# Combining attention heads in parts, and retention outputs one slot later, in a hybrid transformer block

## The chip, the cores and the metric

One core of one Trainium2 chip. The metric is the device time in microseconds of the program, lower is better. An execution's time has a span, from the first to the last instruction that the profiler shows, and a little around it.

## What is computed

One block of a decoder on x of 1 x 1024 x 1024, in fp32. Cut to what matters here:

```python
xn = rmsnorm(x, norm1_g)
qa, ka, va, qr, kr, vr, gr, gate_a, gate_b = split(xn @ w_in)
# mixer A: 12 heads of 128 = 3 groups (dilation 1, 4, 16) x 4 head slots
for gi, (window, dilation) in enumerate(ATT_GROUPS):
    o, lse = dilated_group(qa[gi], ka[gi], va[gi], slopes[gi], window, dilation)
alpha = softmax(stack(lses), axis=0)                 # over the three groups
o_a = sum(alpha[..., None] * stack(outs), axis=0)    # 1024 x 512: one head per slot
# mixer B: 4 heads, q and k of 256, v of 512, in 8 chunks of 128 rows
s = einsum('bnqhd,bnkhd->bnhqk', qc, kc) * decay     # within the chunk
inner = einsum('bnhqk,bnkhv->bnqhv', s, vc)
cross = q_i @ state                                  # from the chunks before
state = state * g_chunk + kz_i.T @ v_i
o_r = head_groupnorm(inner + cross, ret_gn_g, ret_gn_b) * silu(gr)
y = sigmoid(gate_a) * (o_a @ w_proj_a) + sigmoid(gate_b) * (o_r @ w_proj_b)
x = x + y @ w_out
x = x + square(relu(rmsnorm(x, norm2_g) @ w_up)) @ w_down
```

## The kernel before

**Products.** Each fp32 operand is split into a high part, rounded to TensorE's fp32r format by ScalarE (L287), and the rest, computed by VectorE (L288). A product is three matmuls a term: high by high, low by high, high by low; all stand in one helper and show as L193. Nearly all of TensorE's time goes there.

**Slots.** `Pipe.step` emits one such group of matmuls, a slot. Other functions are due at a slot (`pipe.at(lag, fn)`); `step` spreads those due over its terms, so the small matmuls and transposes of earlier rows stand between the large ones, and the engines beside TensorE have time for what lies between. TensorE executes in the order in which the program is traced. On VectorE (DVE), ScalarE (ACT) and SyncE (SP, whose queue issues the DMAs) a list scheduler sets the order from dependencies, buffers and modelled times; `tc.keep_in_program_order(ins)` ties an instruction to the one traced before it on its engine.

**Attention.** 12 heads, one group of one slot each, in the order of the list `heads`: groups 0, 1, 2 for the first three slots and 1, 2, 0 for the last. A head is 8 slots of TensorE, one for a block of 128 rows (8 terms, 24 matmuls of 128x384 for q, k and v). Behind a block: ScalarE sums the squares, VectorE and GpSimd make 1/rms (ssa, L296 and L297), VectorE scales q and k (qk, L601), TensorE turns them a slot later (tr, L607), and ScalarE and VectorE copy them to qT and kT (L611). `attend` adds scores (L532), Exp on ScalarE (pr, L539), the turn of it (L545), pT (L547) and the values (L552, L554). It runs 2 slots behind the block for group 0, which needs only near rows, and 9 slots behind for the groups 1 and 2, whose rows are regrouped by dilation: these end in the next head. The result `acc` of a head, with its maximum and sum, is stored to acc_d in DRAM (L560 to L566) when its last block is done.

**Combination.** When all three groups of a slot are in DRAM, `load_heads` loads half of the rows as four DMAs into `at` (L400), which has one buffer; `combine` makes the weights w (L408 to L419, with an Exp on ScalarE at L412) and mixes the groups into oa (L422, L424, three instructions for each of four blocks of 128 rows); `turn` transposes it, and it is stored to oa_d. For the slots 0 to 2 this happens in the heads 5, 8 and 11: the halves are traced at the blocks 0 and 3, each with all its instructions at once, the first load at block 6 of the head before and the second right behind the first half. Slot 3 is combined in the first head of retention, at the chunks 1 and 4.

**Retention.** 4 heads of 8 chunks. A slot computes v of a chunk (8 terms of three 128x512 matmuls), split into vh and vl. Due in the next slot: `output` (the scores s by v, then q by the state; L193 on ms), its group norm (L799 to L804) and `update` (two matmul groups into ms, then the state St at L816 and its split Sh, Sl); `decay` of the slot's own chunk is due there too (scores, times the mask at L771, split into smh and sml; q into qh, ql; k turned and scaled into kzh, kzl). `turn_o` is due one slot later: it turns the output, gates it by sr (L831) and stores it to on_d. The mask, the scales rc and the norm's gain gng are loaded at the start of this phase (L724 to L729).

**pa.** Behind retention, the combined attention output is multiplied by w_proj_a: 16 slots of 4 terms, each result gated by s, loaded from sg_d (L870) into a ring of four buffers, multiplied (L888) and stored to pa_d (L889). Here `load_o` loads the rows of on_d (oraw, two buffers) and splits them: four rows at the start, four at once as soon as nothing is due any more.

Of the kernel before, what the change touches and what calls it, by code (L numbers as in the profile page):

```python
# [237 lines left out]
def hybrid_block(ctx: ExitStack, tc: tile.TileContext, a: dict, out: bass.AP):  # L238
# [53 lines left out]
    ident = const.tile([P, P], F, name="ident")  # L292

# [10 lines left out]
    heads = [(slot, g) for slot in range(SLOTS) for g in ((0, 1, 2) if slot < SLOTS - 1 else (1, 2, 0))]  # L304
# [91 lines left out]
    def load_heads(s, i, p2b):  # L396
        at = p2b.tile([P, 4, 3, DH + 2], F, name="at", bufs=1)
        rows = acc_d[512 * i:512 * i + 512].rearrange("(t p) (g s) e -> s p t g e", p=P, s=SLOTS)
        for t in range(4):
            nc.sync.dma_start(at[:, t], rows[s, :, t])  # L400
        return at

    def combine(s, i, p2b, at):

        w = p2b.tile([P, 6, 4], F, name="w")
        nm = [at[:, :, g, DH] for g in range(3)]
        dn = [at[:, :, g, DH + 1] for g in range(3)]
        nc.vector.tensor_tensor(w[:, 5], nm[0], nm[1], op=OP.min)  # L408
        nc.vector.tensor_tensor(w[:, 5], w[:, 5], nm[2], op=OP.min)
        for g in range(3):  # L410
            nc.vector.tensor_tensor(w[:, g], w[:, 5], nm[g], op=OP.subtract)
        nc.scalar.activation(w[:, 0:3], w[:, 0:3], AF.Exp)  # L412
# [7 lines left out]
        oa = p2b.tile([P, 4, DH], F, name="oa")  # L420
        for t in range(4):
            nc.vector.tensor_scalar(oa[:, t], at[:, t, 0, :DH], w[:, 0, t:t + 1], None, op0=OP.mult)  # L422
            for g in (1, 2):
                nc.vector.scalar_tensor_tensor(oa[:, t], at[:, t, g, :DH], w[:, g, t:t + 1], oa[:, t],  # L424
                                               op0=OP.mult, op1=OP.add)

        def turn():
            pt = tr.tile([P, 4, P], F, name="tr")
            for t in range(4):
                nc.tensor.transpose(pt[:, t, :], oa[:, t, :], ident)  # L430
            ot = p2b.tile([P, 512], F, name="oaT")
            nc.scalar.activation(ot, pt.rearrange("p t q -> p (t q)"), AF.Copy)
            nc.sync.dma_start(oa_d[s, :, 512 * i:512 * i + 512], ot)

        return turn
# [6 lines left out]
    with ExitStack() as ph:  # L442
# [69 lines left out]
        for head, (slot, g) in enumerate(heads):  # L512
# [57 lines left out]
            for b in range(NT):  # L570
# [8 lines left out]
                if head in (4, 7, 10) and b == 6:  # L579
                    at = load_heads(head // 3 - 1, 0, cmb)  # L580
                if head in (5, 8, 11) and b in (0, 3):
                    pipe.at(3, combine(head // 3 - 1, b // 3, cmb, at))
                    if b == 0:
                        at = load_heads(head // 3 - 1, 1, cmb)
# [133 lines left out]
    with ExitStack() as ph:  # L718
# [4 lines left out]
        maskT = cp.tile([P, RH, P], F, name="maskT")  # L723
        nc.sync.dma_start(maskT, a["c_mask"])  # L724
        rc = const.tile([P, 3, RH], F, name="rc")
        nc.sync.dma_start(rc, a["c_ret"])

        gng = cp.tile([P, 2, NF], F, name="gng")
        nc.sync.dma_start(gng, a["ret_gn"])  # L729
        ready = {}  # L730

        def load_chunk(n):
# [8 lines left out]
            sr = p2.tile([P, 4, P], F, name="sr", bufs=3)  # L741
# [13 lines left out]
        for h in range(RH):  # L755
# [4 lines left out]
            for c in range(NT):  # L760
# [5 lines left out]
                def decay(c=c, h=h, it=it, qT=qT, kT=kT):  # L766
# [5 lines left out]
                    it["s"] = p2.tile([P, P], R, name="smh"), p2.tile([P, P], R, name="sml")  # L772
                    split(*it["s"], sm)
                    if c > 0:
                        it["q"] = p2.tile([P, 2, P], R, name="qh"), p2.tile([P, 2, P], R, name="ql")
                        split(*it["q"], qT)
                    if c < NT - 1:
# [3 lines left out]
                        kzh = p2b.tile([P, 2, P], R, name="kzh")  # L781
                        kzl = p2b.tile([P, 2, P], R, name="kzl")
# [57 lines left out]
                it["v"] = p2.tile([P, DV], R, name="vh"), p2.tile([P, DV], R, name="vl")  # L840
# [13 lines left out]
    with ExitStack() as ph:  # L854
# [21 lines left out]
        load_o(oS, 0)  # L876
        for d in range(KT):
            ua, = W.take(1)
            uh, ul = W[ua]
            for cs in halves():  # L880
# [9 lines left out]
                if ES is None and not pipe.due:  # L890
# [3 lines left out]
                    load_o(as_rows(ES[0]) + as_rows(ES[1]), 4)  # L894
# [313 lines left out]
```

## Time and profile before

| | us |
|---|---|
| median of three runs | 2324.09 (2323.64 to 2328.1) |
| the profiled execution | 2327.33 |
| its span | 2325.6 |
| TensorE (PE) busy | 2281.0 |
| VectorE (DVE) busy | 1165.8 |
| ScalarE (ACT) busy | 926.2 |
| mean granted TensorE clock | 0.995 |

How to read what follows: a row of the timeline gives start, duration, engine, line, operation, out<-in, shape, and in brackets the time that the engine was idle before it and what released it. A row of a group gives, behind the first bar, total busy time and the mean of one in ns, and behind the second the idle time before the group and its releasers. A row of windows gives a stretch from:to and its length, then busy time (and instructions) of PE, PEld, DVE, ACT and POOL, the granted TensorE clock, the DMA engines' share and GB/s. SPq is SyncE's queue issuing a DMA.

### The profile page before, as it was taken

Reading aid. Unit: us, or ns where it says so; the run is one execution under the profiler, and the core shown is the slowest. Engines: PE = TensorE matmul, PEld = TensorE weight load, DVE = VectorE, ACT = ScalarE, POOL = GpSimd, SP = SyncE. Lnnn points to the kernel's source line nnn. Section 1 sums busy time; section 2 is a strip of 40 time slices with the busy share of each in tenths; the row PEclk is TensorE's granted clock in tenths of the full one; section 3 lists DMA queues with packets and bytes.
Section 4 is the critical chain, followed back from the end, with each engine's and each line's share of the span. In section 5 each row is a group of like instructions: output and inputs, shape, how many; then the busy total and the mean of one; then the engine's idle time right before and its main releaser. Section 6 shows DMA issues by size and latency. Waiting matters only on the chain. (4 is left out here: it accounts for less than half of the span.)

```text
span 2325.6 us, 29822 instructions
## 1 busy us (share of the span) xinstructions
PE 2281.0 (98%) x11060; PEld 1952.9 (84%) x11060; DVE 1165.8 (50%) x2356; ACT 926.2 (40%) x2078; POOL 104.0 (4%) x148
## 2 busy tenths in 40 slices
PE   8999999999999999989999999999999999999999
PEld 7999998998888888868888878888788888888887
DVE  6344445454644445557676752363855555233532
ACT  6444444445343333335455533122566666211010
POOL 1111111110000000000000000000000000000000
PEclk9999999999999999999999999999999999999999
DMA  4212322332233333363433385554254457733601
GB/s 140 82 55 74 105 63 78 96 105 91 68 112 112 117 113 109 100 187 104 123 113 100 104 273 180 164 171 163 83 173 166 167 169 271 288 127 133 234 28 73
DMA packets 186275, 303.19 MB, mean 130 GB/s; under 512 B 13457, under 2 KB 99601, under 8 KB 182034
## 3 DMA queue, kind: packets, MB, share of 16 engines
q1 hardware_dynamic: 186130, 301.29, 39.9%
q8 instruction: 87, 1.43, 0.3%
q14 instruction: 58, 0.48, 0.1%
HBM read 204.68 MB, written 96.57 MB: 130 GB/s over the span
## 5 line engine op out<-in xcount | busy, mean ns | idle before, releaser
L193 PE MATMUL mm<-wh,xh 128*128 128x384 f32 (+1 forms) x1536 | 605.1, 394 | 5.1 <-ACT wh L287 5.1
L193 PE MATMUL mm<-wh,xl 128*128 128x384 f32 (+1 forms) x1536 | 561.7, 366 | 2.4 <-DVE xl L288 2.1
L288 DVE TENSOR_TENSOR wl<-raw,wh 128x1024 fp32r<-128x1024 f32 (+2 forms) x282 | 306.6, 1092 | 423.1 <-ACT wh L287 420.1
L193 PE MATMUL mm<-wl,xh 128*128 128x384 f32 (+1 forms) x1344 | 486.6, 362 | 2.6 <-DVE wl L288 2.6
L287 ACT ACTIVATE wh<-raw 128x1024 fp32r<-128x1024 f32 (+2 forms) x282 | 267.2, 953 | 535.7 <-PE mm L193 272.1
L193 PEld LDWEIGHTS mm<-wh,xh 128*128 128x128 f32 x1536 | 291.5, 190 | 36.6 <-ACT wh L287 5.7
L193 PEld LDWEIGHTS mm<-wh,xl 128*128 128x128 f32 x1536 | 290.4, 189 | 35.5 <-DVE xl L288 3.4
L193 PE MATMUL mm<-xl,wh 128*128 128x512 f32 x848 | 309.7, 390 | 1.7 <-DVE xl L288 1.7
L193 PE MATMUL mm<-xh,wh 128*128 128x512 f32 x848 | 310.1, 390 | 0.0
L193 PE MATMUL mm<-xh,wl 128*128 128x512 f32 x720 | 280.7, 390 | 0.0
L193 PEld LDWEIGHTS mm<-wl,xh 128*128 128x128 f32 x1344 | 256.3, 191 | 24.8 <-DVE wl L288 3.1
L193 PE MATMUL ms<-xh,wh 128*128 128x512 f32 x604 | 238.6, 395 | 3.9 <-DVE s L888 3.8
L193 PE MATMUL ms<-xh,wl 128*128 128x512 f32 x604 | 235.4, 390 | 0.0
L193 PE MATMUL ms<-xl,wh 128*128 128x512 f32 x604 | 235.3, 390 | 0.0
L193 PEld LDWEIGHTS mm<-xl,wh 128*128 128x128 f32 x848 | 159.5, 188 | 35.2 <-DVE xl L288 2.1
L193 PEld LDWEIGHTS mm<-xh,wh 128*128 128x128 f32 x848 | 159.6, 188 | 33.0
L1109 DVE TENSOR_TENSOR Yd<-Yd,mm 128x512 f32<-128x512 f32 x112 | 76.9, 686 | 172.3 <-PE mm L193 172.0
L193 PEld LDWEIGHTS mm<-xh,wl 128*128 128x128 f32 x720 | 135.4, 188 | 28.1
L193 PEld LDWEIGHTS ms<-xh,wh 128*128 128x128 f32 x604 | 113.5, 188 | 30.1 <-DVE s L888 4.2
L193 PEld LDWEIGHTS ms<-xh,wl 128*128 128x128 f32 x604 | 113.4, 188 | 23.8
L193 PEld LDWEIGHTS ms<-xl,wh 128*128 128x128 f32 x604 | 113.5, 188 | 22.4
L539 ACT ACTIVATE pr<-s,acc 128x128 f32<-128x128 f32 (+1 forms) x96 | 43.1, 449 | 149.2 <-DVE acc L537 136.9
(187 smaller groups left out, 2756.4 us busy)
## 6 DMA issues: line engine op xcount, KB each, us to landing
h_d<-hs SPq DMA_DIRECT2D x64, 512.0 KB, 3.9
raw<-in_w_att SPq DMA_DIRECT2D x48, 384.0 KB, 3.9
raw<-in_w_up SPq DMA_DIRECT2D x32, 512.0 KB, 3.9
raw<-in_w_down SPq DMA_DIRECT2D x32, 512.0 KB, 4.4
xh<-h_d SPq DMA_DIRECT2D x12, 1024.0 KB, 7.1
xl<-h_d SPq DMA_DIRECT2D x12, 1024.0 KB, 8.7
sg_d<-sg SPq DMA_DIRECT2D x32, 256.0 KB, 2.0
raw<-in_w_rqk_q SPq DMA_DIRECT2D x16, 512.0 KB, 3.6
```

Of the source, the lines that this page charges most:

```text
L193: self.nc.tensor.matmul(ps, x, y, start=start, stop=stop, skip_group_check=not first)
L287: nc.scalar.activation(dst_h, src, AF.Copy)
L288: nc.vector.tensor_tensor(dst_l, src, dst_h.bitcast(F), op=OP.subtract)
L539: nc.scalar.activation(st["p"][:, :n], s[:, :n], AF.Exp, bias=acc[:, b, DH:DH + 1], accum_out=acc[:, b, DH + 1:DH + 2])
L1109: nc.vector.tensor_tensor(Y[:, t, ns], Y[:, t, ns], pm, op=OP.add)
```

## The change

Three things.

**Attention.** The groups run in the order 1, 2, 0 in every slot, so group 0, with its short lag, is last. The combination becomes a list of parts: `weigh` (all of w), four `mix` (one block of 128 rows each), and `turn_mixed`. For a finished slot the first half is loaded at block 6 of the first head of the next slot and the second at block 6 of the second head; `weigh` of the halves is traced at block 1 of the second and of the third head, and one part follows in each block (`mix_next`). The four loads, the first instruction of `weigh` and the first of each `mix` are kept in program order. For slot 3 the same happens in the retention heads 0 and 1 (load at chunk 1, parts from chunk 3).

**Retention.** `output` and `update` are due a slot later, and so is `turn_o` (two for the last two chunks). sr gets four buffers instead of three, and smh, sml, qh, ql, kzh, kzl, vh, vl three instead of two. The mask, rc and gng move to the pool that is kept throughout, with their loads traced right behind attention; a tile `rest` is reserved and not used.

**pa.** `load_o` loads one row in each slot from a list `waiting`, which the second four rows join when nothing is due any more.

```diff
-    heads = [(slot, g) for slot in range(SLOTS) for g in ((0, 1, 2) if slot < SLOTS - 1 else (1, 2, 0))]
+    heads = [(slot, g) for slot in range(SLOTS) for g in (1, 2, 0)]
...
-            nc.sync.dma_start(at[:, t], rows[s, :, t])
+            tc.keep_in_program_order(nc.sync.dma_start(at[:, t], rows[s, :, t]))
...
+        st = {}
+        return [lambda: weigh(p2b, at, st), *(lambda t=t: mix(t, at, st) for t in range(4)),
+                lambda: turn_mixed(s, i, p2b, st)]
+
+    def weigh(p2b, at, st):
+        w = st["w"] = p2b.tile([P, 6, 4], F, name="w")
+        st["o"] = p2b.tile([P, 4, DH], F, name="oa")
...
-        nc.vector.tensor_tensor(w[:, 5], nm[0], nm[1], op=OP.min)
+        tc.keep_in_program_order(nc.vector.tensor_tensor(w[:, 5], nm[0], nm[1], op=OP.min))
...
+    def mix(t, at, st):
+        w, oa = st["w"], st["o"]
+        tc.keep_in_program_order(
+            nc.vector.tensor_scalar(oa[:, t], at[:, t, 0, :DH], w[:, 0, t:t + 1], None, op0=OP.mult))
+        for g in (1, 2):
+            nc.vector.scalar_tensor_tensor(oa[:, t], at[:, t, g, :DH], w[:, g, t:t + 1], oa[:, t],
+                                           op0=OP.mult, op1=OP.add)
...
+    mixing = []
+
+    def mix_next():
+
+        if mixing:
+            mixing.pop(0)()
+            if len(mixing) == 1:
+                pipe.at(1, mixing.pop())
...
-                if head in (4, 7, 10) and b == 6:
-                    at = load_heads(head // 3 - 1, 0, cmb)
-                if head in (5, 8, 11) and b in (0, 3):
-                    pipe.at(3, combine(head // 3 - 1, b // 3, cmb, at))
-                    if b == 0:
-                        at = load_heads(head // 3 - 1, 1, cmb)
+                if head >= 3:
+                    i = head % 3
+                    if i < 2 and b == 6:
+                        at = load_heads(head // 3 - 1, i, cmb)
+                    if i > 0 and b == 1:
+                        mixing = combine(head // 3 - 1, i - 1, cmb, at)
+                    mix_next()
...
+    nc.sync.dma_start(maskT, a["c_mask"])
+    nc.sync.dma_start(rc, a["c_ret"])
+    nc.sync.dma_start(gng, a["ret_gn"])
...
-                pipe.at(0, output, update)
-                pipe.at(1, turn_o)
-                if h == 0 and c in (0, 2):
-                    at = load_heads(SLOTS - 1, c // 2, p2b)
-                if h == 0 and c in (1, 4):
-                    pipe.at(3, combine(SLOTS - 1, c // 4, p2b, at))
+                pipe.at(1, output, update)
+                pipe.at(2 if h < RH - 1 or c < NT - 2 else 3, turn_o)
+                if h < 2:
+                    if c == 1:
+                        at = load_heads(SLOTS - 1, h, p2b)
+                    if c == 3:
+                        mixing = combine(SLOTS - 1, h, p2b, at)
+                    mix_next()
...
-        load_o(oS, 0)
+        waiting = [(place, n) for n, place in enumerate(oS)]
...
-                    load_o(as_rows(ES[0]) + as_rows(ES[1]), 4)
+                    waiting += [(place, 4 + n) for n, place in enumerate(as_rows(ES[0]) + as_rows(ES[1]))]
+                if waiting:
+                    place, n = waiting.pop(0)
+                    load_o([place], n)
```

Where this moves instructions, at three places. VectorE in the head after a finished slot, around the first instruction of w (L408 before, L419 after; ssa and qk belong to a block of that head, kT to the block before it). Before:

```order
L611 TENSOR_SCALAR kT<-tr,gk 128x4x32
L296 TENSOR_SCALAR ssa<-ssa 128x2
L601 TENSOR_TENSOR qk<-mm,ssa 128x256
L408 TENSOR_TENSOR w<-at 128x4
L409 TENSOR_TENSOR w<-w,at 128x4
L411 TENSOR_TENSOR w<-w,at 128x4 x2
```

VectorE at the same place, after:

```order
L622 TENSOR_TENSOR qk<-mm,ssa 128x256
L632 TENSOR_SCALAR kT<-tr,gk 128x4x32
L419 TENSOR_TENSOR w<-at 128x4
L420 TENSOR_TENSOR w<-w,at 128x4
L300 TENSOR_SCALAR ssa<-ssa 128x2
L422 TENSOR_TENSOR w<-w,at 128x4 x3
L622 TENSOR_TENSOR qk<-mm,ssa 128x256
L424 TENSOR_TENSOR w<-w,at 128x4
```

The first instruction of w stood behind a block's qk, and now stands ahead of a block's ssa and qk.

SyncE's queue, around the load of the mask; at the start of retention before (sr_d, rqT, rkT: stores and loads of retention's operands; raw: weights; oar, at: attention's outputs):

```order
L693 DMA sr_d<-sg 128x512
L740 DMA rqT<-rqk_d 128x2x128
L146 DMA raw_9497<-in_w_rv 128x1024
L693 DMA sr_d<-sg 128x512
L740 DMA rkT<-rqk_d 128x2x128
L752 DMA oar<-oa_d 128x1024
L724 DMA maskT<-in_c_mask 128x512
L729 DMA gng<-in_ret_gn 128x32
L400 DMA at<-acc_d 128x3x130 x4
```

SyncE's queue around the same load after, which is at the kernel's start (xt: rows of x):

```order
L146 DMA raw_263<-in_w_att 128x768
L146 DMA raw_269<-in_w_att 128x768
L478 DMA xt<-in_x 128x1024 x3
L650 DMA maskT<-in_c_mask 128x512
L651 DMA rc<-in_c_ret 128x12
L652 DMA gng<-in_ret_gn 128x32
L146 DMA raw_647<-in_w_att 128x768
```

The constants have left the start of retention and stand behind the first rows of x.

VectorE at the end of retention (xh, xl from oraw: the split of rows of on_d; on, st: the norm of an output; onT: its gating). Before:

```order
L288 TENSOR_TENSOR vl<-mm,vh 128x512
L288 TENSOR_TENSOR xh<-oraw,xh 128x1024
L288 TENSOR_TENSOR xl<-oraw,xl 128x1024
L831 TENSOR_TENSOR onT<-onT,sr 128x512
L799 BN_STATS st<-on 128x6
L800 BN_AGGR st<-st 128x2
L801 TENSOR_SCALAR st<-st,rc 128x1
L803 TENSOR_SCALAR st<-st,rc 128x1
L804 TENSOR_SCALAR on<-on,st 128x512
```

VectorE at the end of retention, after (L835 is St, L850 onT, L818 to L822 the norm):

```order
L288 TENSOR_TENSOR vl<-mm,vh 128x512
L288 TENSOR_TENSOR xh<-oraw,xh 128x1024
L850 TENSOR_TENSOR onT<-onT,sr 128x512
L818 BN_STATS st<-on 128x6
L288 TENSOR_TENSOR xl<-oraw,xl 128x1024
L819 BN_AGGR st<-st 128x2
L835 SCALAR_TENSOR_TENSOR St<-St,ms 128x512
L820 TENSOR_SCALAR st<-st,rc 128x1
L835 SCALAR_TENSOR_TENSOR St<-St,ms 128x512
L822 TENSOR_SCALAR st<-st,rc 128x1
L288 TENSOR_TENSOR Sl<-St,Sh 128x512
```

The last update of the state (L835 and Sl) now stands behind the last vl, among the splits of the rows of on_d.

More of the change, by code (lines that the diff above doesn't have):

```diff
@@ L292, in hybrid_block @@
     ident = const.tile([P, P], F, name="ident")
+    maskT = const.tile([P, RH, P], F, name="maskT")
+    rc = const.tile([P, 3, RH], F, name="rc")
+    gng = const.tile([P, 2, NF], F, name="gng")
+    const.tile([P, 224], F, name="rest")
     def rsqrt(dst, src, scale):
@@ L419, in combine, with turn_mixed @@
             nc.vector.tensor_tensor(w[:, g], w[:, g], w[:, 4], op=OP.mult)
-        oa = p2b.tile([P, 4, DH], F, name="oa")
-        for t in range(4):
[L422 to L435, printed above, removed]
+    def mix(t, at, st):
[5 more added lines that the diff above has]
+                                           op0=OP.mult, op1=OP.add)
+    def turn_mixed(s, i, p2b, st):
+        pt = tr.tile([P, 4, P], F, name="tr")
+        for t in range(4):
+            nc.tensor.transpose(pt[:, t, :], st["o"][:, t, :], ident)
+        ot = p2b.tile([P, 512], F, name="oaT")
+        nc.scalar.activation(ot, pt.rearrange("p t q -> p (t q)"), AF.Copy)
+        nc.sync.dma_start(oa_d[s, :, 512 * i:512 * i + 512], ot)
+    mixing = []
[4 more added lines that the diff above has]
+                pipe.at(1, mixing.pop())
     attn = ExitStack()
@@ L721, in hybrid_block @@
         p2b = pool(ph, "p22b", 2, "right")
[L723 to L729, printed above, removed]
         ready = {}
@@ L740, in load_chunk @@
                 nc.sync.dma_start(qk[i], rqk_d[h, i, :, :, ts].rearrange("f p t -> p f t"))
-            sr = p2.tile([P, 4, P], F, name="sr", bufs=3)
+            sr = p2.tile([P, 4, P], F, name="sr", bufs=4)
             nc.sync.dma_start(sr, sr_d[4 * h:4 * h + 4, :, ts].rearrange("f p t -> p f t"))
@@ L771, in decay @@
                     nc.vector.tensor_tensor(sm, sp[:, :P], maskT[:, h, :], op=OP.mult)
-                    it["s"] = p2.tile([P, P], R, name="smh"), p2.tile([P, P], R, name="sml")
+                    it["s"] = p2.tile([P, P], R, name="smh", bufs=3), p2.tile([P, P], R, name="sml", bufs=3)
                     split(*it["s"], sm)
                     if c > 0:
-                        it["q"] = p2.tile([P, 2, P], R, name="qh"), p2.tile([P, 2, P], R, name="ql")
+                        it["q"] = p2.tile([P, 2, P], R, name="qh", bufs=3), p2.tile([P, 2, P], R, name="ql", bufs=3)
                         split(*it["q"], qT)
@@ L780, in decay @@
                             nc.tensor.transpose(pt[:, f, :], kT[:, f], ident)
-                        kzh = p2b.tile([P, 2, P], R, name="kzh")
-                        kzl = p2b.tile([P, 2, P], R, name="kzl")
+                        kzh = p2b.tile([P, 2, P], R, name="kzh", bufs=3)
+                        kzl = p2b.tile([P, 2, P], R, name="kzl", bufs=3)
                         nc.scalar.activation(kzh, pt[:, :2], AF.Copy, scale=rc[:, 2, h:h + 1])
@@ L839, in hybrid_block @@
                     pm = values(us, ts, c == NT - 1)
-                it["v"] = p2.tile([P, DV], R, name="vh"), p2.tile([P, DV], R, name="vl")
+                it["v"] = p2.tile([P, DV], R, name="vh", bufs=3), p2.tile([P, DV], R, name="vl", bufs=3)
                 split(*it["v"], pm)
-                pipe.at(0, output, update)
-                pipe.at(1, turn_o)
-                if h == 0 and c in (0, 2):
-                    at = load_heads(SLOTS - 1, c // 2, p2b)
-                if h == 0 and c in (1, 4):
-                    pipe.at(3, combine(SLOTS - 1, c // 4, p2b, at))
+                pipe.at(1, output, update)
[6 more added lines that the diff above has]
+                    mix_next()
                 if h == RH - 1 and c >= 4:
@@ L893, in hybrid_block @@
                     ES = [slot_of(ext) for _ in range(3)] + [slot_of(pool(e1, "ext1", 1, "right"))]
-                    load_o(as_rows(ES[0]) + as_rows(ES[1]), 4)
+                    waiting += [(place, 4 + n) for n, place in enumerate(as_rows(ES[0]) + as_rows(ES[1]))]
+                if waiting:
+                    place, n = waiting.pop(0)
+                    load_o([place], n)
+        assert not waiting
         other = places + as_rows(ES[2]) + as_rows(ES[3])
@@ L1196 @@
     from concourse.bass_utils import run_bass_kernel_spmd as _run
-    nc = _bacc.Bacc("TRN2", target_bir_lowering=False, num_devices=1)
+    nc = _bacc.Bacc("TRN2", target_bir_lowering=False, num_devices=1, dynamic_dma_scratch_size=1024)
     arrays, aps = {}, {}
```

1 line of the change is left out of this document (removed).

## The prediction

> **What bounds the kernel now.** I read the page first, then the busy time by stretches of 100 us, then TensorE's own timeline at the places where it falls short, and last the clock in narrow stretches there. Of the page, the span and the engines:
>
> ```profile
> span 2325.6 us, 29822 instructions
> PE 2281.0 (98%) x11060; PEld 1952.9 (84%) x11060; DVE 1165.8 (50%) x2356; ACT 926.2 (40%) x2078; POOL 104.0 (4%) x148
> ```
>
> TensorE (PE) is busy 2281.0 of 2325.6 us: 44.6 us of idle time, and what half clock costs, are all that an edit of order can win. Busy time by stretch (columns: sum, PE, PEld, DVE, ACT, POOL, granted clock, DMA share, GB/s) shows where that lies:
>
> ```profile
> 200.00:300.00 100.00, 96.92 (x583) 94.48 (x582) 44.10 (x174) 40.25 (x165) 12.46 (x18) 0.98 0.32 91
> 300.00:400.00 100.00, 95.22 (x580) 92.41 (x579) 44.74 (x180) 39.74 (x167) 12.45 (x18) 0.98 0.26 72
> 400.00:500.00 100.00, 96.86 (x584) 93.79 (x582) 49.40 (x188) 44.85 (x176) 12.56 (x18) 0.98 0.34 99
> 1000.00:1100.00 100.00, 91.37 (x421) 74.70 (x420) 66.00 (x167) 46.12 (x91) 5.09 (x6) 0.95 0.48 145
> 1300.00:1400.00 100.00, 94.14 (x426) 75.48 (x425) 61.95 (x104) 41.01 (x72) 3.81 (x5) 1.00 0.65 208
> ```
>
> These are the heads 5, 8 and 11 of attention (where finished slots are combined), the start of retention, and its end with the stage pa behind it. TensorE's timeline there, each row with the idle time before it and its releaser:
>
> ```profile
> 230.53 0.44 PE L193 MATMUL mm<-wh,xh 128*128 128x384 f32 x1 [1.67 <-ACT wh L287]
> 232.26 0.44 PE L193 MATMUL mm<-wl,xh 128*128 128x384 f32 x1 [1.29 <-DVE wl L288]
> 364.57 0.45 PE L193 MATMUL mm<-wh,xh 128*128 128x384 f32 x1 [3.44 <-ACT wh L287]
> 366.30 0.69 PE L193 MATMUL mm<-wl,xh 128*128 128x384 f32 x1 [1.29 <-DVE wl L288]
> 480.42 0.46 PE L552 MATMUL ms<-Vd,pT 128*128 128x128 f32 x2 [1.54 <-DVE pT L547]
> 482.35 0.69 PE L545 MATMUL ms<-ident,pr 128*128 128x128 f32 x2 [0.41 <-ACT pr L539]
> 495.92 0.44 PE L545 MATMUL ms<-ident,pr 128*128 128x128 f32 x2 [1.09 <-ACT pr L539]
> 1032.63 0.80 PE L193 MATMUL ms<-vh,smh 128*128 128x512 f32 x1 [8.47 <-ACT smh L287]
> 1347.80 0.44 PE L825 MATMUL tr<-ident,on 128*128 128x128 f32 x2 [0.69 <-DVE on L804]
> 1374.61 0.50 PE L193 MATMUL ms<-xh,wh 128*128 128x512 f32 x1 [2.91 <-DVE s L888]
> ```
>
> Two groups cover scattered waits: the retention outputs' second matmul (on vl) and the pa stage (on s, the row of 2.91 included):
>
> ```profile
> L193 PE MATMUL ms<-vl,smh 128*128 128x512 f32 x32 | 13.2, 413 | 2.0 <-DVE vl L288 2.0
> L193 PE MATMUL ms<-xh,wh 128*128 128x512 f32 x604 | 238.6, 395 | 3.9 <-DVE s L888 3.8
> ```
>
> Behind some of these waits TensorE runs at half clock (the column after POOL):
>
> ```profile
> 232.90:236.40 3.50, 3.50 (x13) 3.50 (x12) 2.92 (x12) 1.12 (x4) 0.73 (x1) 0.51 0.81 219
> 366.00:369.50 3.50, 3.20 (x11) 3.11 (x12) 2.95 (x11) 1.14 (x7) 0.70 (x1) 0.51 0.56 149
> 478.00:482.00 4.00, 2.40 (x13) 1.76 (x12) 3.57 (x17) 0.31 (x1) 0.44 (x1) 1.00 0.00 0
> 482.00:485.50 3.50, 3.15 (x12) 3.16 (x12) 1.94 (x8) 1.55 (x10) 0.69 (x1) 0.51 0.49 116
> 1032.00:1038.50 6.50, 5.87 (x14) 4.62 (x15) 3.56 (x14) 1.30 (x4) 0.56 (x1) 0.50 0.43 114
> ```
>
> Work at half clock takes twice its time, so each of these stretches loses half of its PE time besides the wait.
>
> **Combining in parts, groups in one order.** Before, the second half's first instruction (L408) waits at the head of VectorE's queue for its load; behind it, ScalarE's Exp of w (L412) waits, and behind that the split of the next weights, for which TensorE waits:
>
> ```profile
> 336.86 0.52 SPq L566 DMA_DIRECT2D acc_d<-acc  x1
> 348.85 0.17 DVE L408 TENSOR_TENSOR w<-at 128x4 f32<-128x4 f32 x1 [5.92 <-DMA at<-acc_d]
> 362.82 0.17 DVE L408 TENSOR_TENSOR w<-at 128x4 f32<-128x4 f32 x1 [5.61 <-DMA at<-acc_d]
> 229.53 0.21 ACT L412 ACTIVATE w<-w 128x12 f32<-128x12 f32 x1 [6.21 <-DVE w L411]
> 229.65 1.56 ACT L287 ACTIVATE wh<-raw 128x768 fp32r<-128x768 f32 x2
> ```
>
> The second load gets its buffer only when the first half is mixed; in the change the two halves lie a head apart, so this wait has no cause left. In head 11 it was VectorE itself (busy 3.57 of the 4.00 us to 482) that kept pT and pr: 16 oa instructions in a row. Split into four turns of one block each, they leave room. Removed: 1.67+1.29+3.44+1.29+1.54+0.41+1.09 = 10.73 us idle, and (3.50+3.20+3.15)/2 = 4.9 of half clock: 15.65 us.
>
> Added: the first `weigh` of a slot floats forward in VectorE's queue, ahead of a block's ssa and qk in the head after the slot (the order below the change shows it). The data it needs now ends with group 0, whose last block is stored in the next head. Rows of before for such a block, and for that qk and its turn on TensorE:
>
> ```profile
> 210.74 0.28 ACT L554 ACTIVATE acc<-ms 128x128 f32<-128x128 f32 x1 [1.04 <-PE ms L552]
> 222.91 0.16 DVE L296 TENSOR_SCALAR ssa<-ssa 128x2 f32<-128x2 f32 x1
> 223.94 0.42 DVE L601 TENSOR_TENSOR qk<-mm,ssa 128x256 f32<-128x256 f32 x1 [0.87 <-POOL ssa L297]
> 224.80 0.38 PE L607 MATMUL tr<-ident,qk 128*128 128x128 f32 x2
> ```
>
> From store to `w` took 348.85-336.86 = 12.0 us. So here: acc done at 211.02, w at 223.0, two w instructions 0.34, then ssa to the end of qk 224.36-222.91 = 1.45: 224.8, just when TensorE wants the turn at 224.80. Slack is nothing; behind the waiting w stand ssa, qk and kT, and TensorE waits for them. Nearest rows: zero (it lands a little sooner) and the 3.44 of before. I take 0.5 each, 1.5 for three slots. The second `weigh` loads some three blocks ahead of use and waits for nothing. Head 11 keeps one combination beside its blocks: 0.4 left of 1.54+0.41+1.09 (choice; between 0 and all). Gain: 15.65-1.5-0.4 = 13.75.
>
> **Constants kept, output a slot later: the start.** The first output waits for the mask's load, which SyncE issues behind the loads of chunks and weights:
>
> ```profile
> 1027.36 0.33 SPq L724 DMA_DIRECT2D maskT<-in_c_mask  x1
> 1031.94 0.29 DVE L771 TENSOR_TENSOR sm<-ms,maskT 128x128 f32<-128x128 f32 x1 [2.30 <-DMA maskT<-in_c_mask]
> ```
>
> In the change the mask is issued behind the loads of x, a thousand us before use, and output 0 stands a slot later, with the values of a whole chunk between. So 8.47 and half of 5.87 (2.9) go: 11.4; I leave 0.3 for decay 0, which still follows its own load (between 0 and the 2.30 of that wait). Gain 11.1. Early in the kernel three small loads join SyncE behind x; the loads of weights behind them come far ahead of use, so nothing.
>
> **The slots of retention.** vh and vl are made a slot ahead now, so the 2.0 us of the vl group go. Each slot holds the same instructions, and an update stands as far ahead of the output that reads its state as before. Cost nothing; cover: the eight terms of values between. Gain 2.0.
>
> **The end of retention, and pa.** The waits are 0.69 (on) and 3.8 (s): 4.5. Loads of on_d spread one a slot, and turn_o later, speak for their going. Two things speak against. Update 30 and output 31, which had stood in a slot of values, come into the first two pa slots, 4 terms of 3 matmuls instead of 8. Between them the state passes VectorE, behind splits of the loaded rows:
>
> ```profile
> L816 DVE SCALAR_TENSOR_TENSOR St<-St,ms 128x512 f32<-128x512 f32 x48 | 32.7, 681 | 0.0
> L288 DVE TENSOR_TENSOR Sl<-St,Sh 128x512 fp32r<-128x512 f32 x56 | 38.4, 686 | 0.0
> L288 DVE TENSOR_TENSOR xl<-oraw,xl 128x1024 fp32r<-128x1024 f32 x8 | 9.8, 1222 | 8.2 <-ACT xl L287 8.2
> ```
>
> Two St and two Sl make 2.7 us, one split ahead of them 1.2: 3.9, against 2 pa terms (6 matmuls of 0.395, 2.4): 1.5 us late. I take 1.4 (0 to 3.9, when nothing covers it). And the buffers of s still turn through store, load and use:
>
> ```profile
> 1362.41 0.90 SPq L889 DMA_DIRECT2D pa_d<-s  x2
> 1373.87 1.44 DVE L888 TENSOR_TENSOR s<-s,ms 128x512 f32<-128x512 f32 x2 [4.76 <-DMA s<-sg_d]
> ```
>
> From that store to the sum that uses the buffer again 11.5 us pass, of which VectorE waited 4.76; the change keeps this ring of four. Of 3.8 I leave 1.5 (0 to 3.8). Gain 4.5-1.4-1.5 = 1.6.
>
> **Sum.** 13.75+11.1+2.0+1.6 = 28.4 us of 2325.6. The profiled execution took 2327.33 us, 3.24 over the median of 2324.09 (three runs, 2323.64 to 2328.1); the terms are differences, so they are taken from the median: 2295.7 us. About 0.2%, 4.6 us, is what can be told from no change.
>
> A rule is weighed here. The stretch 478 to 482 held 1.6 us of idle in pieces, the longest 1.54, and half clock came behind it. The Trainium skill ("TensorE: Matmul & The Clock Gate", section "What's actually happening") has the clock halve after at least one idle window of some 3.4 us. By that, only the stalls of 3.44 and 8.47 explain theirs; this trace disagrees, at 482 as at 232.9.
>
> **The rivals.** *Weigh stalls TensorE all the same.* Should group 0's rows land 2 us later than in slot 1's load, each of three slots waits 2.0 us and pays half of a 3.2 us stretch: 3 x 3.6 = 10.8 instead of 1.5, so 2305.0. For it: slack of nothing, and the 5.92 that w waited; against: the 12.0 us already hold a store, four loads behind it and their way. Chance 0.13.
>
> *The end gives it back.* State and ring at their far ends, 3.9+3.8 for 1.4+1.5: 4.8 less, 2300.5. For it: TensorE has half the cover there. Chance 0.10.
>
> *All of it goes*, w, state and ring hidden: 15.65+11.4+2.0+4.5 = 33.5, 2290.6. Chance 0.17.
>
> *Half clock has another cause than pieces of idle.* Then the stretches at 232.90 and 482.00 stay at 0.51 though their waits go: (3.50+3.15)/2 = 3.3 less, 2299.0. Against it: both stand right behind waits. That would be the page's rule; chance 0.04.
>
> *Slower.* Outputs a slot later hold sm, q, kz and v a slot longer; should three buffers fall short, VectorE and ScalarE wait in every one of 31 slots for an output to release them. At 1.2 us a slot that is 37.2-28.4 = 8.8 over: 2332.9; slower by over 0.2% from (28.4+4.6)/31 = 1.07 us a slot. Against it: three buffers for a distance of two slots. Chance 0.03.
>
> **How the numbers follow.** The forecast has 0.53. The range of 2289 to 2306 reaches from a little under "all" to a little over the first rival's 2305.0; outside lie the slower case, a first rival with more than 2 us of delay, and two rivals together. Only the slower case, and half clock with several losses together, come near no change: faster 0.94, same 0.03, slower 0.03.
>
> **What would show it.** Right: rows on wh and wl at the heads 5 and 8 without idle time; no 8.47; granted clock 1.00 from 200 to 500 and at 1032; the group on vl at 0. Wrong: qk or tr waiting 2 us or more in the head after a slot; St, Sh or Sl named ahead of output 31; waits on kz, smh or qh in each slot of retention, or a sum of gains under 18 us.

## The result, and the profile after

The changed kernel took 2289.83 us (four runs, 2288.66 to 2290.57) beside 2323.86 for the kernel before (four runs) on the same chip: 34.0 us less, a ratio of 0.9849 (95% interval 0.9832 to 0.9866). The forecast was 2295.7, 28.4 less. On the chips of the later runs the kernel before took 2319 to 2320; the changed kernel, repeated there, gained 31.6 (0.9858, 0.9843 to 0.9873). Differences below are against the runs of before made together with each kernel.

The page of the changed kernel: span and engines.

```profile
span 2286.9 us, 29817 instructions
PE 2266.9 (99%) x11060; PEld 1948.3 (85%) x11060; DVE 1166.6 (51%) x2356; ACT 923.4 (40%) x2078; POOL 103.1 (5%) x148
```

TensorE's idle time fell from 44.6 to 20.0 us, and its busy time by 14.1, though it executes the same 11060 matmuls: 7.8 of that is the half clock of the prediction's terms (4.9 and 2.9). The stretches that were short before (same columns as in the prediction; the granted clock is the column after POOL):

```profile
200.00:300.00 100.00, 99.79 (x629) 97.38 (x628) 48.06 (x187) 44.99 (x189) 12.41 (x18) 1.00 0.25 73
300.00:400.00 100.00, 99.79 (x619) 97.56 (x618) 52.30 (x203) 45.99 (x187) 13.10 (x19) 1.00 0.32 96
400.00:500.00 100.00, 99.97 (x617) 98.03 (x615) 44.89 (x174) 41.65 (x176) 13.81 (x20) 1.00 0.32 95
1000.00:1100.00 100.00, 99.31 (x485) 82.32 (x484) 72.09 (x173) 53.53 (x113) 7.09 (x9) 1.00 0.54 158
1300.00:1400.00 100.00, 97.68 (x435) 79.93 (x434) 51.82 (x70) 39.03 (x56) 1.65 (x3) 1.00 0.76 246
```

All are at full clock, and nearly full. What the changed kernel still waits for there, on TensorE's timeline:

```profile
500.82 0.70 PE L552 MATMUL ms<-kT,qT 128*128 128x256 f32 x2 [0.85 <-DVE pT L567]
1005.43 0.68 PE L788 MATMUL ms<-rqT,rkT 128*128 128x128 f32 x4 [0.69 <-DMA rkT<-rqk_d]
1308.97 0.50 PE L193 MATMUL ms<-xh,wh 128*128 128x512 f32 x1 [1.17 <-DVE St L835]
1351.41 0.50 PE L193 MATMUL ms<-xh,wh 128*128 128x512 f32 x1 [1.03 <-DVE s L909]
```

And the group on vl:

```profile
L193 PE MATMUL ms<-vl,smh 128*128 128x512 f32 x32 | 12.7, 396 | 0.0
```

So the waits on wh and wl, the 8.47 on smh, and the 2.0 on vl are gone, and 3.7 us in four waits stand in their place, each about where the prediction put one (head 11, decay 0, the state at the end, s in pa). The first w, which the prediction charged 0.5 a slot, costs nothing. Its chain in the first finished slot (ScalarE's last acc of group 0, SyncE's store and load, VectorE's w and qk, TensorE's turn):

```profile
165.56 0.28 ACT L574 ACTIVATE acc<-ms 128x128 f32<-128x128 f32 x1 [1.04 <-PE ms L572]
165.86 0.38 SPq L580 DMA_DIRECT2D acc_d<-acc  x1
170.54 1.57 SPq L404 DMA_DIRECT2D at<-acc_d  x2
176.58 0.17 DVE L419 TENSOR_TENSOR w<-at 128x4 f32<-128x4 f32 x1 [4.58 <-DMA at<-acc_d]
177.89 0.43 DVE L622 TENSOR_TENSOR qk<-mm,ssa 128x256 f32<-128x256 f32 x1 [0.59 <-POOL ssa L301]
179.64 0.38 PE L628 MATMUL tr<-ident,qk 128*128 128x128 f32 x2
```

VectorE does wait 4.58 us at w, with ssa and qk behind it, as foretold. But w starts 10.7 us after the store, not 12.0. qk ends at 178.32, and TensorE wants it at 179.64: 1.3 us of slack. In the third finished slot w came latest, 11.4 us after the store, and 0.6 us were left (store, w, qk, turn):

```profile
419.48 0.38 SPq L580 DMA_DIRECT2D acc_d<-acc  x1
430.89 0.17 DVE L419 TENSOR_TENSOR w<-at 128x4 f32<-128x4 f32 x1 [5.28 <-DMA at<-acc_d]
432.21 0.42 DVE L622 TENSOR_TENSOR qk<-mm,ssa 128x256 f32<-128x256 f32 x1 [0.59 <-POOL ssa L301]
433.26 0.38 PE L628 MATMUL tr<-ident,qk 128*128 128x128 f32 x2
```

The 12.0 of the prediction was the longest of three such rows in its own trace. In the first slot of the kernel before it was 11.3 us, in the third 11.7; the first:

```profile
204.94 0.52 SPq L566 DMA_DIRECT2D acc_d<-acc  x1
216.26 0.17 DVE L408 TENSOR_TENSOR w<-at 128x4 f32<-128x4 f32 x1 [5.23 <-DMA at<-acc_d]
```

Over all the profiles kept, the time from the last store to a slot's first w was 9.7 to 12.0 us where attention is as before (group 2 is stored last, eight profiles) and 10.2 to 11.4 us where it is changed (group 0, twelve profiles). It varies from slot to slot and from execution to execution; a difference between the groups does not show.

To see where the time went, take the start of the same matmul of L193, counted from the first, in two traces: the 2689th lies behind attention, the 5761st behind pa.

| | to the 2689th | from there to the 5761st | rest |
|---|---|---|---|
| before, first profile | 636.29 | 758.45 | 930.8 |
| after, first profile | 616.26 | 740.73 | 929.9 |
| before, second profile | 634.74 | 755.02 | 929.8 |
| after, second profile | 615.98 | 740.26 | 930.1 |
| forecast of the difference | -13.75 | -14.7 | 0 |

Attention gave 20.0 and 18.8 us, retention with pa 17.7 and 14.8. Both profiles of before are long in attention: in the profiles of six other kernels below whose attention is as before, the 2689th comes at 632.4 to 633.0 us, and beside those the changed kernel gained 16 to 17.

### The profile page after: what moved, and what is told of

Same layout as the page of the kernel before. It is cut to its first block, busy times and chain, and to the rows that moved or that the text cites. A ratio compares the mean times of both kernels' runs of the same rounds, so it can differ in the third digit from the quotient of the medians.

```text
span 2286.9 us, 29817 instructions
## 1 busy us (share of the span) xinstructions
PE 2266.9 (99%) x11060; PEld 1948.3 (85%) x11060; DVE 1166.6 (51%) x2356; ACT 923.4 (40%) x2078; POOL 103.1 (5%) x148
## 4 chain that ended last, share of the span: by engine, by line
PE 93%; DMA 2%; DVE 2%; ACT 1%; issue 1%; POOL 0%; SPq 0%; POOLq 0%; DVEq 0%; ACTq 0%
PE mm L193 66%; PE ms L193 20%; PE ms L572 1%; PE ms L552 1%; PE tr L628 1%; DMA pa_d<-s 1%; PE ms L565 1%; PE ms L788 1%; PE tr L844 1%; DMA acc_d<-acc 0%; DVE xl L288 0%; ACT xh L287 0%; DVE xn L1047 0%; PE tr L799 0%; DMA s<-sg_d 0%
## 5 line engine op out<-in xcount | busy, mean ns | idle before, releaser
L193 PE MATMUL mm<-wh,xh 128*128 128x384 f32 (+1 forms) x1536 | 602.1, 392 | 0.0
L193 PE MATMUL mm<-wh,xl 128*128 128x384 f32 (+1 forms) x1536 | 559.3, 364 | 1.7 <-DVE xl L288 1.6
L193 PE MATMUL mm<-wl,xh 128*128 128x384 f32 (+1 forms) x1344 | 483.4, 360 | 0.0
L193 PEld LDWEIGHTS mm<-wh,xl 128*128 128x128 f32 x1536 | 288.9, 188 | 33.9 <-DVE xl L288 2.6
L193 PEld LDWEIGHTS mm<-wh,xh 128*128 128x128 f32 x1536 | 290.0, 189 | 30.2
L193 PE MATMUL mm<-xl,wh 128*128 128x512 f32 x848 | 309.8, 390 | 1.7 <-DVE xl L288 1.7
L193 PE MATMUL mm<-xh,wh 128*128 128x512 f32 x848 | 310.2, 390 | 0.0
L193 PE MATMUL mm<-xh,wl 128*128 128x512 f32 x720 | 280.6, 390 | 0.0
L193 PEld LDWEIGHTS mm<-wl,xh 128*128 128x128 f32 x1344 | 254.8, 190 | 21.4
L193 PE MATMUL ms<-xh,wh 128*128 128x512 f32 x604 | 237.9, 394 | 2.2 <-DVE St L835 1.2
L193 PE MATMUL ms<-xh,wl 128*128 128x512 f32 x604 | 235.2, 389 | 0.0
L193 PE MATMUL ms<-xl,wh 128*128 128x512 f32 x604 | 235.2, 389 | 0.0
L193 PEld LDWEIGHTS mm<-xl,wh 128*128 128x128 f32 x848 | 159.6, 188 | 35.1 <-DVE xl L288 2.1
L193 PEld LDWEIGHTS mm<-xh,wh 128*128 128x128 f32 x848 | 159.5, 188 | 33.0
L193 PEld LDWEIGHTS mm<-xh,wl 128*128 128x128 f32 x720 | 135.6, 188 | 28.3
L193 PEld LDWEIGHTS ms<-xh,wh 128*128 128x128 f32 x604 | 113.5, 188 | 25.8 <-DVE St L835 1.6
L193 PEld LDWEIGHTS ms<-xh,wl 128*128 128x128 f32 x604 | 113.4, 188 | 23.7
L193 PEld LDWEIGHTS ms<-xl,wh 128*128 128x128 f32 x604 | 113.5, 188 | 22.6
```

The source lines that it names most:

```text
L193: self.nc.tensor.matmul(ps, x, y, start=start, stop=stop, skip_group_check=not first)
```

## The experiments

**The parts alone.** Four kernels from the one before. The attention part alone (`heads`, `load_heads`, `combine` and its calls as in the change; slot 3 combined in retention as before):

> The kernel before with the attention part of the change alone (groups in the order 1, 2, 0; combination in parts; retention and pa as before). Theory that the terms add and the new waits cost nothing: 15.65 us of idle and half clock go, with a little from waits too short to be listed, so 16 to 17 us faster. Theory that the first w keeps TensorE waiting half a us in each of three slots: 13.7 us. Rival that the attention part holds only the waits and the rest of the gain came from retention: about 11 us.

Measured: 2303.91 beside 2319.39, 15.5 less (0.9931, 0.9914 to 0.9948). Its trace keeps the wait at the start of retention:

```profile
1012.24 0.79 PE L193 MATMUL ms<-vh,smh 128*128 128x512 f32 x1 [8.35 <-ACT smh L287]
```

That is nearest to the first theory, but the interval, 12 to 20 us, holds 13.7 as well. What tells against the half us a slot is the trace: none of the three turns of qk behind w waits. The constants alone:

```diff
+    maskT = const.tile([P, RH, P], F, name="maskT")   # rc, gng too; loads behind attention
...
-    nc = _bacc.Bacc("TRN2", target_bir_lowering=False, num_devices=1)
+    nc = _bacc.Bacc("TRN2", target_bir_lowering=False, num_devices=1, dynamic_dma_scratch_size=1024)
```

> The kernel before with the constants kept throughout alone (their loads early; outputs not later). Theory that the terms add: the wait of 8.47 and 2.9 of half clock go but for 0.5 to 1 that output 0 still waits for its scores, two terms behind them in the same slot: 10.5 to 11 us faster. Rival that both steps are needed, since output 0 follows decay 0 too closely: under 8 us.

Measured: 2324.24, 4.9 more than before (1.0022, 1.0013 to 1.0032): neither theory. The wait on smh was down to 0.37, and the 11 us had been spent elsewhere. With the later output as well (buffers, `pipe.at(1, output, update)`, turn_o):

> The same, and output, update and turn_o a slot later with their buffers. Theory that the terms add: 2.0 us of waits on vl and what was left at output 0 go, 1.2 comes in on the state at the end: 12 to 13 us faster than before, 1 to 2 faster than with the constants alone. Rival of a loss in every slot from buffers held longer: slower than with the constants alone.

Measured: 2320.57 (1.0003, 0.9994 to 1.0012). The wide products from about 590 us on ran slower in both: 44.29 us for 192 matmuls instead of 43.52, at full clock and without idle time. These two kernels lacked the tile `rest`. Every kernel with the constants moved, the changed one too, also has the argument `dynamic_dma_scratch_size=1024` of the cut above; no run has it by itself. The loads of on_d, one row in a slot of pa, alone:

> The kernel before with only the rows of on_d loaded one in a slot of pa. Theory that their loads held up those of s: of the 3.8 us of waits on s some 2 to 3 go, 2 to 3 us faster. Rival that SyncE's order hardly changes, and the later output is what thins the loads in pa: within 1 us of before.

Measured: 2320.94 (1.0004, 0.9995 to 1.0013). The rival holds: loading a row a slot shows no gain by itself.

**The tile rest.** The same two kernels with `const.tile([P, 224], F, name="rest")`, and the changed kernel without it:

> The kernel before with the constants kept throughout, this time with the tile rest, which puts all tiles behind the constants 12 KB lower than before (a multiple of 4096 bytes). Theory that the earlier run of this step lost its gain because its tiles lay 896 bytes off (1.8% in the wide products from 590 to 1970 us): the wide products are back at 43.52 us for 192 matmuls, and 10.5 to 11 us are gained over before. Rival that the early constants themselves slow the products or bring nothing: again no faster than before.

> The same, and output, update and turn_o a slot later with their buffers, pa as before. Theory that the terms add: waits on vl (2.0) go, and most of pa's on s go with the thinner loads: 2 to 4 us faster than the run with the constants alone, 13 to 15 faster than before. Rival of a loss in every slot: slower than with the constants alone.

> The changed kernel without the tile rest: nothing else differs, but all tiles behind it lie 896 bytes lower. Theory that addresses matter: the wide products take 44.2 us for 192 matmuls instead of 43.52, and 14 to 15 us of the gain are lost, so about 20 us faster than before. Rival that the loss in the two runs had another cause: as fast as the changed kernel, 34 us faster than before.

Measured, beside 2318.98: 2310.16 (8.8 less; 0.9967, 0.9954 to 0.998), 2307.0 (12.0 less; 0.995, 0.9935 to 0.9965) and 2302.51 (16.5 less; 0.9931, 0.9915 to 0.9948). So early constants bring 8.8, a little under what was expected, the later output 3.2 more, as expected, and without the unused tile half of the change's gain is lost. Then the tile was made longer, by 512 (352 instead of 224 elements), 256 (288) and 128 bytes (256):

> The changed kernel with the unused tile 512 bytes longer. If the wide products' speed goes by addresses modulo 512 bytes or less, nothing changes: 43.52 us for 192 matmuls, the changed kernel's time. If it goes by 1024, 2048 or 4096: up to 14 us slower, 44.2 us for 192 matmuls.

> The changed kernel with the unused tile 256 bytes longer. If the products' speed has a period of 256 bytes in the address: the changed kernel's time, 43.52 us for 192 matmuls. If the period is 512: up to 14 us slower, up to 44.2 us for 192 matmuls.

> The changed kernel with the unused tile 128 bytes longer, which is where the kernel without it lies if the period is 256 bytes: then 14 us slower and 44.2 us for 192 matmuls. If the period is 512, this place has not been tried, and any loss from 0 to 14 us may come.

Measured: 2287.43 (0.9861, 0.9846 to 0.9875), 2288.04 (0.9859, 0.9842 to 0.9875) and 2302.53 (0.9923, 0.9908 to 0.9938). One stretch of 100 us amid the wide products in the changed kernel (second profile), without the tile, with 128 bytes more and with 256 bytes more; what counts is the number of matmuls in the first pair of brackets:

```profile
700.00:800.00 100.00, 100.00 (x443) 82.83 (x442) 44.69 (x55) 33.93 (x48) 0.00 (x0) 1.00 0.36 111
```

```profile
700.00:800.00 100.00, 100.00 (x435) 81.38 (x434) 44.20 (x56) 32.96 (x47) 0.00 (x0) 1.00 0.34 108
```

```profile
700.00:800.00 100.00, 100.00 (x435) 81.37 (x434) 44.22 (x55) 32.76 (x47) 0.00 (x0) 1.00 0.35 108
```

```profile
700.00:800.00 100.00, 100.00 (x443) 82.84 (x442) 44.50 (x55) 33.93 (x48) 0.00 (x0) 1.00 0.35 111
```

443 or 435 matmuls, each time on a TensorE that is 100% busy at full clock. Lengths that differ by 256 and 512 bytes are alike; 128 bytes more, or 896 less (which is 128 modulo 256), cost 1.8% of the rate.

**Mask late, output late.** The changed kernel with the loads of the constants put behind `load_chunk(3)`:

```diff
                 load_chunk(NT * h + c + 2)
+                if h == 0 and c == 1:
+                    tc.keep_in_program_order(nc.sync.dma_start(maskT, a["c_mask"]))
```

> The changed kernel with the loads of the mask, rc and gng put back behind the loads of the first chunks, where the mask lands after decay 0 has been computed. Theory that the later output alone covers the mask: within 2 us of the changed kernel, 32 to 34 us faster than before, and no wait over 1 us on smh. Rival that the gain of 11 hangs on the early load: a wait of some 5 to 8 us comes back at the start of retention, and 23 to 28 us faster than before.

Measured: 2294.2 beside 2318.98, 24.8 less (0.9895, 0.988 to 0.991): the rival, with a wait a little shorter than it had. TensorE's row, and the two stretches around it:

```profile
1014.08 0.59 PE L193 MATMUL ms<-vh,smh 128*128 128x512 f32 x1 [4.37 <-ACT smh L287]
```

```profile
1009.70:1014.30 4.60, 0.23 (x2) 0.22 (x2) 1.58 (x5) 1.16 (x5) 0.00 (x0) 1.00 0.90 240
1014.30:1017.80 3.50, 3.50 (x9) 2.73 (x9) 2.22 (x7) 1.25 (x4) 0.23 (x1) 0.51 0.97 280
```

A slot of cover takes 4 of the 8.4 us away, not all; the early load is needed for the rest.

**The wait at w.** The changed kernel again, and two in which all of the first `weigh` stands ahead of ssa of the same block (block 5 of the head after the slot), or of block 4's:

```diff
+                ahead = head >= 3 and (head % 3, b) == (0, 5)
+                if ahead:
+                    at = load_heads(head // 3 - 1, 0, cmb)
+                    mixing = combine(head // 3 - 1, 0, cmb, at)
+                    mix_next()
-                rsqrt(ss[:, 2:4], ss[:, 0:2], 1.0 / DH)
+                rsqrt(ss[:, 2:4], ss[:, 0:2], 1.0 / DH, ahead)
```

> The changed kernel once more, on the chip of the runs that follow. If the parts add up (16 for attention, 12 for constants and later output, 2 to 4 for pa behind the later output): 30 to 32 us faster than before on this chip, where before takes some 5 us less than on the first. Rival that the parts are worth more together: 34 or more.

> The changed kernel with all of the first weigh of a slot put ahead of ssa of the same block (block 5 of the head after the slot) on VectorE, its load just ahead of it; in the changed kernel ssa and qk of that block stand between the first instructions of w and are done 1.3 us before TensorE turns them. Theory that this slack of 1.3 us is all that hides the wait: qk comes 1.5 us late in each of three slots, 4.5 us slower than the changed kernel, up to 10 if half clock follows each. Rival that TensorE's other work hides more: no slower.

> The same one block earlier: w then waits for its data while two blocks' qk stand behind it. Theory: qk of block 4, wanted at 175.2 on the clock of the changed kernel's profile, is ready at 181.1: 5.9 us a slot, 17.6 for three, and half of 3.4 us of half clock behind each, 22 to 23 us slower than the changed kernel. Rival that the wait is bounded by less than a block: under 10 us slower.

Measured, beside 2319.42: 2287.78 (31.6 less), 2290.88 (0.9873, 0.9858 to 0.9888) and 2309.3 (0.9952, 0.9937 to 0.9967): 3.1 and 21.5 us slower than the changed kernel. At block 5 the three turns of qk wait 0.78, 0.66 and 0.38 us, so the loss is nearer to the theory's 4.5 than to none; its last 1.3 us are not traced to a wait. The turn of qk in the first slot, at block 5 and at block 4, and the clock behind the latter:

```profile
181.44 0.41 PE L635 MATMUL tr<-ident,qk 128*128 128x128 f32 x2 [0.78 <-DVE qk L629]
```

```profile
180.70 0.66 PE L635 MATMUL tr<-ident,qk 128*128 128x128 f32 x2 [4.59 <-DVE qk L629]
```

```profile
178.10:185.00 6.90, 4.30 (x15) 4.33 (x16) 3.51 (x18) 1.06 (x6) 0.75 (x2) 0.51 0.00 1
```

The mechanism of the first rival is real: at block 4 it makes three stalls of 4.59, 5.15 and 4.95 us, with half clock behind each. In the changed kernel's first profile it lies 0.6 to 1.3 us away.

**Split or spacing.** The changed kernel with each half combined in one go:

```diff
-                        mixing = combine(head // 3 - 1, i - 1, cmb, at)
-                    mix_next()
+                        parts = combine(head // 3 - 1, i - 1, cmb, at)
+                        for part in parts[:-1]:
+                            part()
+                        pipe.at(3, parts[-1])
```

> The changed kernel with each half combined in one go (weigh and all four mix at block 1, the turn three slots later), the halves still a head apart. Theory that it is the spacing of the halves that took away the waits: within 3 us of the changed kernel, the second halves in the heads of group 0 costing up to 1 each. Rival that the split into parts made it, as the waits of pT and pr in head 11 of the kernel before suggest (3.0 and half clock of 1.6 there, now in each of three heads of group 0): 9 to 14 us slower.

Measured: 2292.69 beside 2319.81, 27.1 less (0.9884, 0.9869 to 0.9898), some 4.5 us of the changed kernel's gain. The loss is not where either theory had it, in the second halves or on pT and pr, but in the first halves, where the split of the next weights comes behind the oa instructions on VectorE; second finished slot:

```profile
313.11 0.44 PE L193 MATMUL mm<-wl,xh 128*128 128x384 f32 x1 [1.36 <-DVE wl L288]
```

The other two slots have 0.92 and 1.49 us there. So the split made the last 4.5 us of attention's gain, and the rest is due to the spacing of the halves together with the order 1, 2, 0 of the groups; no run has one of these two without the other.

**The rest without attention; the kernel before once more; a better end.** All of the change but attention and the spreading of slot 3's combination over two heads of retention, from the kernel before:

> The kernel before with all of the change but the attention part: constants kept (with the tile rest), output a slot later, rows of on_d loaded one a slot. Theory that the parts add and that pa gains only with both: 12 us for constants and later output and up to 3 more, 12 to 15 us faster than before; with attention's 16 that makes the 31.6 of the whole. Rival that load_o gives nothing: the same 12 as without it.

Measured: 2307.71 (12.1 less; 0.995, 0.9932 to 0.9968), what it was without the spread loads. With attention's 15.5 that makes 27.6; the whole gains 31.6, which the intervals of the parts, some 4 us either way, allow. One piece is in neither part: slot 3's combination. Where it stands in one head of retention, as here, VectorE runs twelve oa instructions in a row, and TensorE then waits for a norm:

```profile
1046.89 0.66 PE L827 MATMUL tr<-ident,on 128*128 128x128 f32 x4 [1.50 <-DVE on L806]
```

The changed kernel has no such wait; what this piece brings was not run by itself. And before, profiled again:

> The kernel before, unchanged, profiled once more. Theory that the first profile's waits vary by execution: attention's waits differ by some 2 us from the 10.7 of the first profile, and the second profile is 3 to 8 us shorter than the first (2325.6). Rival that they are fixed: the same waits within 0.3 us.

Measured: the same time as its companions, with a span of 2319.5. Its waits at the places of the prediction:

```profile
232.04 0.44 PE L193 MATMUL mm<-wl,xh 128*128 128x384 f32 x1 [1.29 <-DVE wl L288]
362.49 0.44 PE L193 MATMUL mm<-wh,xh 128*128 128x384 f32 x1 [3.56 <-ACT wh L287]
364.22 0.69 PE L193 MATMUL mm<-wl,xh 128*128 128x384 f32 x1 [1.30 <-DVE wl L288]
491.02 0.46 PE L552 MATMUL ms<-Vd,pT 128*128 128x128 f32 x2 [1.69 <-DVE pT L547]
1369.95 0.50 PE L193 MATMUL ms<-xh,wh 128*128 128x512 f32 x1 [0.17 <-DVE s L888]
```

Attention's larger waits add up much as in the first, but the 1.67 at head 5 and its half clock are absent, and where pa had waited 2.91 stands 0.17. So waits behind DMAs differ from execution to execution; these two spans differ by 6 us. Last, the changed kernel with output 31 and its turn another slot later, and six buffers for s with five loaded ahead instead of three:

```diff
-                pipe.at(1, output, update)
+                pipe.at(1 if h < RH - 1 or c < NT - 1 else 2, output, update)
...
-        pm2 = pool(load, "pm2", 4)
+        pm2 = pool(load, "pm2", 6)
```

> The changed kernel with the last output (and its turn) another slot later, so that the state has a whole slot between update 30 and output 31, and with six buffers for s in pa instead of four. Theory: the wait of 1.17 on the state and of 1.03 on s go, 2 us faster than the changed kernel. Rival that the wait on s is set by the DMA engines' load rather than by the ring: 1 us faster, the wait on s stays.

Measured: 2286.66 (0.9857, 0.984 to 0.9873) beside the changed kernel's 2287.78. The waits on St and s went; a new one came at output 31:

```profile
1313.29 0.50 PE L193 MATMUL ms<-vh,smh 128*128 128x512 f32 x1 [0.80 <-DVE s L909]
```

1.1 us, within the two kernels' spreads (2286.41 to 2289.09 and 2287.2 to 2288.25): not shown to be faster.

## Why the prediction was right or wrong

**Right: what goes.** Each wait that was to go went, with its half clock, and between the first output and the last update no wait came into the slots of retention. The constants' load is needed, the later output removes the vl waits, and the state at the end costs 1.17 for 1.4. Retention and pa gave 14.8 us in the second pair of profiles for 14.7 forecast, and that it fits so well is in part luck: idle time fell by 10.0 us where 11.8 were forecast, half clock by 2.7, and 2.1 are busy time for which the prediction had no term. The 17.7 of the first pair holds the one wait of 2.91 in pa, of which the second profile of before shows that it does not come every time.

**Wrong: attention, "15.65-1.5-0.4 = 13.75".** It was 15.5 in the run by itself, 16 to 17 beside most profiles and 18 to 20 beside the two of before. The step that failed is "From store to w took 348.85-336.86 = 12.0 us. So here", with the 0.5 us a slot charged for it: 12.0 was the longest of three rows at hand, and in the changed kernel's profile it took 10.7, 11.0 and 11.4. That left 0.6 to 1.3 us of slack in each slot, and the 1.5 fell away. The 0.4 left for head 11 was 0.85. "All of it goes" came nearest to the time, and the measured 2289.83 lies at the low end of the range. The runs with w further ahead show that the rival's mechanism was rightly described and its distance misjudged.

That accounts for 1.5 of some 3 us. The rest lies mostly in TensorE's busy time, which the prediction held constant but for half clock, and it is explained only in part. TensorE's busy time from the start to the 2689th matmul, in the second profiles of before and of the changed kernel:

```profile
0.00:634.74 634.74, 613.30 (x3585) 578.29 (x3586) 306.53 (x999) 285.57 (x1014) 72.17 (x108) 0.99 0.28 88
```

```profile
0.00:615.98 615.98, 607.08 (x3585) 575.36 (x3585) 307.43 (x999) 283.96 (x1014) 71.78 (x108) 1.00 0.29 91
```

Idle time falls by 21.4-8.9 = 12.5 us and busy time by 6.2. Of the idle time 2.5 us lie in the first 50 us, ahead of any combination, and differ between executions: TensorE is idle there for 6.7 to 9.8 us in the kernels with attention as before and for 6.4 to 7.8 in those with it changed. Two stretches of half clock explain some 3.3 of the 6.2. The other 2.9 is in matmuls that take a little longer in before. About 1 us of it lies in the first matmul behind a wait, which adds some 0.4 us of busy time where one behind another matmul adds 0.17: there are 15 such in before and 9 in the changed kernel. For the rest, whether it is how waits too short for a row appear, or the new order of the groups, no run tells.

**Not priced: the unused tile.** The prediction gave `rest` no term. That came out right only because the tile is there: the change moves every tile behind the constants, and without the 896 bytes it would have lost some 15 us, half of the forecast.

**The clock.** The rival that half clock has another cause than idle time fell: no stretch of half clock is left where the waits went. When it comes is not settled by the length of a wait alone, as the last section shows.

## What to carry to other kernels

A wait behind a DMA is priced from all rows of its kind, with their spread, and not from one: three rows of 11.3 to 12.0 us stood in the trace, and 0.6 to 1.3 us decided here whether three stalls came or none. Spacing two uses of one buffer, with the order of groups that allows it, did more than splitting the work. And when a change moves tiles in SBUF, compare the rate of the unchanged matmuls first: two steps that did what they should lost all they had won to an address.

## What the runs showed of the hardware

**Addresses.** TensorE's rate depends here on where in SBUF its operands lie relative to each other: up to 1.8% between placements that differ by 128 bytes, and none between those that differ by 256, 512 or 12288 (other distances were not tried). It shows only in the stages in which one operand is in tiles that the longer constants move and the other in tiles that stay: the wide products of 594 to 1000 us and those behind pa, to 1930 us (44.06 to 44.35 us for 192 matmuls against 43.52), while attention, where both move, and the products at the end keep their time. The wide products show it singly. The kernel computes them as seven products, N1 to N7, a unit. The weights move; before 1000 us N1 to N3 read rows of x in tiles that move too, and N4 to N7 rows in tiles that stay. Without the tile `rest`, the twelve matmuls of N4 to N7 take 71 to 80 ns longer than with it in the median, those of N1 to N3 15. At the products with w_up, where N5 reads rows that move, its 80 ns become 15, and N4, N6 and N7 keep their 71 to 72. How the two reads collide was not tried.

**Half clock.** The same wait of 2.80 us in the norm behind the output projection, in two executions of the changed kernel, was followed by half clock once and by full clock once:

```profile
1632.50:1636.00 3.50, 0.70 (x6) 0.51 (x5) 3.50 (x7) 2.30 (x4) 0.00 (x0) 1.00 0.00 0
1636.00:1639.40 3.40, 3.40 (x10) 2.66 (x9) 3.40 (x6) 3.09 (x6) 0.00 (x0) 0.50 0.02 5
```

```profile
1631.80:1635.20 3.40, 0.60 (x6) 0.44 (x5) 3.40 (x7) 2.21 (x4) 0.00 (x0) 1.00 0.00 0
1635.20:1638.60 3.40, 3.40 (x17) 2.69 (x15) 3.40 (x7) 3.10 (x6) 0.00 (x0) 1.00 0.02 5
```

With the 1.6 us of the prediction, in pieces, that were followed by half clock, this speaks for a share of idle time in a window whose start does not follow the kernel. The granted clock of the 20 profiles kept here bears it out. In each of them every change of clock lies on one grid of 3.413 us, and the grid lies elsewhere in each execution. Cut by its grid, the wait of 2.80 us falls into one window in the first execution and is shared by two in the second:

```profile
1632.55:1635.97 3.42, 0.62 (x6) 0.48 (x5) 3.42 (x7) 2.22 (x4) 0.00 (x0) 1.00 0.00 0
```

```profile
1629.87:1633.28 3.41, 2.12 (x12) 1.41 (x10) 3.41 (x6) 1.74 (x4) 0.00 (x0) 1.00 0.44 177
1633.28:1636.69 3.41, 1.90 (x11) 1.67 (x12) 3.41 (x7) 2.47 (x5) 0.00 (x0) 1.00 0.02 5
```

Of all such windows at full clock, the 27 in which the profile has TensorE busy for less than 1.4 us were each followed by half clock, of the 30 with 1.49 to 1.73 us 6 were, and of those with more none. The Trainium skill ("TensorE: Matmul & The Clock Gate", section "What's actually happening") has such a free-running window of about 3.4 us. Its "idle window", if that means one idle throughout, is what these rows contradict, since TensorE was busy 0.62 us in the window before half clock.
